# A strided-slice copy: gpsimd's transfers go over four batches, 1 MB each, and the hardware queues load eight pairs in place of six

## The chip, the cores and the metric

One core of one Trainium2 chip. The metric is the device time of one execution in microseconds (us). A run is an execution; most kernels here have three to nine runs, the four that measure one kind of transfer have one (state unknown). Runs more than 1.5% above the fastest of the same kernel count as slow and are left out of the ratios. A ratio is always the mean time of one kernel's fast runs over that of the other's fast runs of the same rounds, so it is not quite the ratio of the medians that stand beside it. Each profile is of one execution. Sizes of a batch or a transfer (2 MB, 1 MB, 512 KB) are in powers of two; totals and GB/s are decimal.

The engines that compute (tensor, vector, scalar, gpsimd) do nothing here but issue transfers. The work is done by the core's 16 DMA engines. Transfers are put to them on three queues: those of sync and of scalar, called the hardware queues (q1 and q10 in the profile), and that of gpsimd (q0, which the profile calls software_dynamic). The profile records what they move in packets, here of 2 or 4 KB of data.

## The reference

```python
# x: (32, 1024, 512) float32, start 0, stop 512, stride 2
def reference(x, start, stop, stride):
    return x[:, start:stop:stride, :].astype(np.float32)
```

The result is 32 batches of 256 rows of 2 KB: row r of a batch is input row 2r. 16.78 MB are read and 16.78 MB written. A batch of the input is 2 MB, a batch of the output 0.5 MB, so two batches n apart are 2n MB apart in the input and n/2 MB in the output.

## The kernel before

Every batch is split into its even and its odd output rows. One half goes direct from input to output on gpsimd's queue; the other half is loaded into on-chip tiles ("held") and stored from there by sync. Which half goes direct is decided by `apart`.

```python
FIRST = 6

def apart(b):                        # parity of the rows of batch b that go direct
    return 1 - (b >> 1 & 1)

def two(t, b, step, parity):         # rows of one parity of batches b and b + step: 512 KB
    return t[b : b + step + 1 : step].rearrange("b (p two) d -> two p b d", two=2)[parity]

    # ...
    copied = [(g + b, step) for g in range(0, B, 8) for b, step in ((0, 5), (2, 5), (1, 3), (3, 3))]
    # ...
            for i in range(FIRST):                       # six pairs on the hardware queues
                (sp, act)[i % 2].dma_start(held[i], two(src, 2 * i, 1, 1 - apart(2 * i)))
            for n, (b, step) in enumerate(copied):       # 16 direct pairs, 10 held ones
                pool.dma_start(two(out, b, step, apart(b)), two(src, b, step, apart(b)))
                i = n + FIRST // 2
                if FIRST <= i < pairs:
                    pool.dma_start(held[i], two(src, 2 * i, 1, 1 - apart(2 * i)))
            order = [pairs - 3, *range(pairs - 3), pairs - 2, pairs - 1]
            for b in (2 * i + k for i in order for k in range(2)):   # 32 stores of 256 KB
                to = out[b].rearrange("(p two) d -> two p d", two=2)[1 - apart(b)]
                sp.dma_start(to, held[b // 2][:, b % 2])
```

The direct pairs are 3 or 5 batches apart. The parity hangs on bit 1 of the batch number: direct rows are odd in batches 0, 1, 4, 5, 8, ... and even in 2, 3, 6, 7, ... I call this the rule. The direct pairs (0,5), (2,7), (1,4), (3,6) and the held pairs (0,1), (2,3), ... are just pairs whose two batches agree in bit 1, so that one transfer can have one parity.

## Time and profile before

| | before |
|---|---|
| time, median (range) | 79.38 us (79.25 to 80.14), three runs |
| profiled span | 77.1 us |
| bytes moved by the DMA engines | 25.17 MB, mean 327 GB/s |
| sum of the queues' shares of 16 engines | 96.1% |
| gpsimd's transfers | 26 of 512 KB, up to 8 under way |
| hardware transfers | 6 loads of 512 KB, 32 stores of 256 KB |

The prediction shows the lines behind these numbers. In the view by stretches each line has the stretch in us from the span's start and its length, the time in which gpsimd was busy with instructions (and how many), the clock of the tensor engine (idle here), the share of the time in which the 16 DMA engines had a packet, and the bytes moved per time. The share can come out a little over 1, because a packet is counted whole in the stretch in which it starts and because packets overlap a little: in the records up to 22 are under way at once on the 16 engines. A DMA share of 1 beside a low rate means that the engines have work but their packets take long.

### The profile page before, as it was taken

The numbers are of one execution on the slowest core, as the hardware profiler recorded it, in microseconds if no ns is written. First come the engines' busy times: TensorE is split into PE (matmuls) and PEld (weight loads), VectorE is DVE, ScalarE is ACT, GpSimd is POOL, SyncE is SP. The second block draws the span as 40 slices with busy tenths as digits, with TensorE's granted clock in tenths as the row PEclk, the third lists the DMA queues.
The fourth block names the chain that finished last, engine by engine and source line by source line (L and its number), as shares of the span: only waits on it lengthen the run. The fifth ranks groups of instructions, "written<-read, shape, count | busy, mean of one in ns | idle before, by whom it ended". The sixth has DMA issues, their size and how long they took to land.

```text
span 77.1 us, 122 instructions
## 1 busy us (share of the span) xinstructions
POOL 18.6 (24%) x30
## 2 busy tenths in 40 slices
POOL 4996003213436333464633000000000000000000
DMA  0899999999996999999989999999999999999970
GB/s 9 263 303 310 298 310 314 354 327 389 381 327 238 372 340 310 378 378 417 330 319 361 317 342 358 384 333 338 406 406 405 358 350 371 349 350 357 358 245 7
DMA packets 9984, 25.17 MB, mean 327 GB/s; under 512 B 1024, under 2 KB 1024, under 8 KB 9984
## 3 DMA queue, kind: packets, MB, share of 16 engines
q0 software_dynamic: 3744, 13.63, 51.3%
q1 hardware_dynamic: 5424, 9.96, 37.7%
q10 hardware_dynamic: 816, 1.57, 7.1%
HBM read 16.78 MB, written 16.78 MB: 435 GB/s over the span
## 4 chain that ended last, share of the span: by engine, by line
DMA 48%; issue 3%; POOLq 1%; POOL 1%; PEldq 0%
DMA held<-in_x_dram 34%; DMA out_dram<-in_x_dram 14%; POOLq L77 1%; POOL out_dram L39 1%; PEldq L77 0%
## 5 line engine op out<-in xcount | busy, mean ns | idle before, releaser
L39 POOL DMA_DIRECT2D out_dram<-in_x_dram x16 | 11.2, 699 | 11.5 <-DMA out_dram<-in_x_dram 9.9
L42 POOL DMA_DIRECT2D held<-in_x_dram x10 | 7.3, 729 | 11.4 <-DMA out_dram<-in_x_dram 8.0
L63 POOL MEMSET const-float32-0.0<- 128x1 f32 x1 | 0.1, 98 | 0.2 <-issue 0.2
L63 POOL MEMSET const-bfloat16-1.0<- 128x1 bf16 x1 | 0.1, 102 | 0.0
L63 POOL MEMSET const-float32-1.0<- 128x1 f32 x1 | 0.1, 98 | 0.0
L63 POOL MEMSET const-uint8-127<- 128x1 uint8 x1 | 0.1, 98 | 0.0
## 6 DMA issues: line engine op xcount, KB each, us to landing
out_dram<-in_x_dram POOLq DMA_DIRECT2D x16, 512.0 KB, 13.0
out_dram<-held SPq DMA_DIRECT2D x32, 256.0 KB, 6.1
held<-in_x_dram POOLq DMA_DIRECT2D x10, 512.0 KB, 12.4
held<-in_x_dram SPq DMA_DIRECT2D x3, 512.0 KB, 11.2
held<-in_x_dram ACTq DMA_DIRECT2D x3, 512.0 KB, 12.2
```

The lines of the kernel that those rows point to most:

```text
L39: pool.dma_start(two(out, b, step, apart(b)), two(src, b, step, apart(b)))
L42: pool.dma_start(held[i], two(src, 2 * i, 1, 1 - apart(2 * i)))
L63: nc = _bacc.Bacc("TRN2", target_bir_lowering=False, num_devices=1)
L77: with _tile.TileContext(nc) as tc:
```

## The change

gpsimd's transfers go over four batches at once, 1 MB each, so that there are fewer of them and fewer waits; and eight pairs, not six, are loaded by the hardware queues, which then carry 40 transfers. The core of the diff:

```diff
-FIRST = 6
+EARLY = 4
+
+def batches(q):
+    first = q // 4 * 16 + q % 4
+    return [first + 4 * k for k in range(4)]
 
-def apart(b):
-    return 1 - (b >> 1 & 1)
+def apart(q):
+    return 1 - (q >> 1 & 1)
 
-def two(t, b, step, parity):
-    return t[b : b + step + 1 : step].rearrange(...)[parity]
+def part(t, q, parity, of=slice(0, 4)):
+    b = batches(q)[of]
+    return t[b[0] : b[-1] + 1 : 4].rearrange(...)[parity]
...
+            for q in range(EARLY):
+                for queue, of in ((nc.sync, slice(0, 2)), (nc.scalar, slice(2, 4))):
+                    queue.dma_start(held[q][:, of], part(src, q, 1 - apart(q), of))
+            direct(0, slice(0, 2))
+            direct(0, slice(2, 4))
+            direct(1)
+            load(4)
+            direct(2)
+            load(5)
+            direct(3)
+            direct(4)
+            load(6)
...
+            for q in [quads - 2, *range(quads - 2), quads - 1]:
+                for k, b in enumerate(batches(q)):
...
```

A quad q is the batches q, q+4, q+8, q+12 (or 16 more). Its batches share bit 1 with q, so `apart(q)` is the old rule for every batch, and the same rows go direct as before. That is also why the step is 4: of four equally spaced batches all agree in bit 1 only if the step is a multiple of 4.

More of the change, by code (lines that the diff above doesn't have):

```diff
@@ L3 @@
 from concourse import mybir
-FIRST = 6
-def apart(b):
-    return 1 - (b >> 1 & 1)
-def two(t, b, step, parity):
-    return t[b : b + step + 1 : step].rearrange("b (p two) d -> two p b d", two=2)[parity]
+EARLY = 4
[6 more added lines that the diff above has]
+    b = batches(q)[of]
+    return t[b[0] : b[-1] + 1 : 4].rearrange("b (p two) d -> two p b d", two=2)[parity]
 def kernel(tc, x, start, stop, stride, out):
@@ L29, with direct, load @@
     P = rows // 2
-    sp, act, pool = nc.sync, nc.scalar, nc.gpsimd
-    copied = [(g + b, step) for g in range(0, B, 8) for b, step in ((0, 5), (2, 5), (1, 3), (3, 3))]
-    pairs = B // 2
+    quads = B // 4
     with tc.tile_pool(name="io", bufs=1) as io:
-        held = [io.tile([P, 2, D], x.dtype, name=f"held{i}") for i in range(pairs)]
-        with tc.manual_schedule():
-            for i in range(FIRST):
-                (sp, act)[i % 2].dma_start(held[i], two(src, 2 * i, 1, 1 - apart(2 * i)))
-            for n, (b, step) in enumerate(copied):
-                pool.dma_start(two(out, b, step, apart(b)), two(src, b, step, apart(b)))
-                i = n + FIRST // 2
-                if FIRST <= i < pairs:
-                    pool.dma_start(held[i], two(src, 2 * i, 1, 1 - apart(2 * i)))
-            order = [pairs - 3, *range(pairs - 3), pairs - 2, pairs - 1]
-            for b in (2 * i + k for i in order for k in range(2)):
-                to = out[b].rearrange("(p two) d -> two p d", two=2)[1 - apart(b)]
-                sp.dma_start(to, held[b // 2][:, b % 2])
+        held = [io.tile([P, 4, D], x.dtype, name=f"held{q}") for q in range(quads)]
+        def direct(q, of=slice(0, 4)):
+            nc.gpsimd.dma_start(part(out, q, apart(q), of), part(src, q, apart(q), of))
+        def load(q):
+            nc.gpsimd.dma_start(held[q], part(src, q, 1 - apart(q)))
+        with tc.manual_schedule():
+            for q in range(EARLY):
[10 more added lines that the diff above has]
+            load(6)
+            direct(5)
+            load(7)
+            direct(6)
+            direct(7)
+            for q in [quads - 2, *range(quads - 2), quads - 1]:
+                for k, b in enumerate(batches(q)):
+                    to = out[b].rearrange("(p two) d -> two p d", two=2)[1 - apart(q)]
+                    nc.sync.dma_start(to, held[q][:, k])
 _INS = ['x', 'start', 'stop', 'stride']
```

## The prediction

> **What bounds the kernel now.** No engine computes anything: the kernel copies every second row of half of each batch, 16.78 MB read and 16.78 MB written. Half goes straight from input to output, half through on-chip tiles ("held"), so the DMA engines carry 8.39 MB three times over (direct, load, store): 25.17 MB. I read first the page's slices and its table of DMA queues.
>
> ```profile
> DMA  0899999999996999999989999999999999999970
> ...
> DMA packets 9984, 25.17 MB, mean 327 GB/s; under 512 B 1024, under 2 KB 1024, under 8 KB 9984
> ...
> q0 software_dynamic: 3744, 13.63, 51.3%
> q1 hardware_dynamic: 5424, 9.96, 37.7%
> q10 hardware_dynamic: 816, 1.57, 7.1%
> ```
>
> The queues' shares sum to 96.1% of 16 engines' span: the DMA engines never rest. q0 is gpsimd's queue, q1 that of sync (three loads, all 32 stores), q10 that of scalar (three loads). The first question about any wait here is therefore whether it ever leaves a DMA engine without work, so I next read the stretches.
>
> ```profile
> core 0: us, POOL busy (x), PEclk, DMA share, GB/s
> 2.00:6.00 4.00, 4.00 (x7) 1.00 0.93 285
> 6.00:18.00 12.00, 2.38 (x4) 1.00 0.99 323
> 18.00:42.00 24.00, 11.32 (x16) 1.00 1.02 348
> 42.00:54.00 12.00, 0.00 (x0) 1.00 1.00 345
> 54.00:60.00 6.00, 0.00 (x0) 1.00 1.05 405
> 60.00:74.00 14.00, 0.00 (x0) 1.00 1.07 355
> ```
>
> From 6 us on the DMA share is 0.99 or more in each. What differs is GB/s, that is, how long one packet takes. The stages are: hardware loads alone (2 to 6), hardware loads beside gpsimd's transfers (6 to 18), gpsimd alone (18 to 42), gpsimd beside stores (42 to 54), stores alone (54 on). The waits of gpsimd come last:
>
> ```profile
> POOL out_dram L39 <- DMA out_dram<-in_x_dram: 9.9, 9, 1.9
> POOL held L42 <- DMA out_dram<-in_x_dram: 8.0, 2, 5.4
> POOL held L42 <- DMA held<-in_x_dram: 3.4, 6, 0.7
> ```
>
> They sum to over 20 us, and the order of instructions shows why: eight transfers go out at once, and each later one waits for the one eight before it. This wait looks as if it were to be won. The stretch 18 to 42, in which nearly all of it falls, says no: the share there is 1.02, since eight transfers of 512 KB (4.2 MB, 12 us at 348 GB/s) stand in the queue while gpsimd waits.
>
> What the time consists of, from the packet records. A 2 KB packet of the hardware queues takes 84 ns undisturbed (the median from 54 to 60 us), a 4 KB packet of gpsimd's queue 159 ns (its median). The means over the run are longer: 13.63 MB in 4 KB packets are 3328, and 51.3% of 77.1 us times 16 over 3328 is 190 ns (some 9 ns a completion packet included); likewise 96 ns in q1 and 114 ns in q10. Undisturbed, the data packets would take (3328 x 159 + 5632 x 84)/16 = 62.6 us. The remaining 11 us of the 74 us are stretching: in the records 6.2 us in q0, 3.2 in q1, 1.4 in q10. In q0 it sits in few packets: 90% take under 194 ns, the worst 1% over 800, and while they last the other queues' packets of that engine stand still. So the bound is how memory answers a mix of reads and writes, not the issue.
>
> **What the Trainium skill says.** "DMA: Bandwidth & Descriptors", section Issuing engines are not separate DMA queues: transfers of all issuers run on the same 16 engines and interleave, and issuing from several only saves issue time. The trace agrees: 16 engines are full at 0.99 to 1.02 with one queue and with three. The same page, section Measured, gives 341 GB/s for 1 MB and asks for at least 1 MiB per transfer. That is for a transfer which stands alone; with eight in the queue this trace gets 348 from 512 KB ones, so I expect nothing from size as such. The same page, section SWDGE vs HWDGE vs iDMA, says that a packet of gpsimd's queue is preferably at most 4096 B. Here all are 4096 B, with two rows of 2 KB in each instruction's inner dimension; no run yet shows whether four rows make one packet of 8 KB. Last, its section Latency and other measured facts has a row on HBM row pitches of large powers of two (a pitch of 2 MiB 164 GB/s, 4 and 8 MiB 103, in copies between HBM tensors). The kernel before pairs batches 1, 3 or 5 apart (2, 6, 10 MB in the input); the new one puts batches 4 apart, 8 MB, into one transfer. No trace of before shows what that costs.
>
> **The change, part by part.**
>
> *Fewer and larger gpsimd transfers.* 26 of 512 KB become 13: two of 512 KB and eleven of 1 MB, 12.58 MB in all. gpsimd has up to 7 MB under way where it had 4.2, and only the last five of 13 wait for a completion. Issue: 26 at 0.70 or 0.73 us become 11 at perhaps double that, the same 18 us or less, all beside the transfers. Removed wait: 0 us on the path, as the engines were full. Completion packets: 26 x 16 become 13 x 16, 208 fewer at 9 ns on 16 engines, 0.1 us gained. The first transfer stays at 512 KB, so the start at 6.4 us (first packet of q0) stays.
>
> *Packet size.* From 84 ns for 2 KB and 159 for 4 KB: 9 ns fixed and 75 ns for each 2 KB, so 8 KB would be an estimated 309 ns (the few 8 KB packets before the kernel's start take 307 at the least). 3072 packets of 4 KB at 159 are 30.5 us of 16 engines, 1536 of 8 KB at 309 are 29.7: 0.8 us gained, if it happens. I give it 4 in 10, so 0.3 us. If stretching comes per packet, part of q0's 6.2 us could go as well; I add 0.4 us for that.
>
> *Two more pairs on the hardware queues.* 1.05 MB of loads move from q0 to q1 and q10. The stage with three queues gets longer: there the hardware queues and q0 share about equally (0.94 + 1.03 MB against 1.91 from 6 to 18 us), so about 2.1 MB go at 323 instead of 348 GB/s: 6.5 - 6.0 = 0.5 us lost.
>
> *When stores start.* The first store waits for pair 13 (at 42.1 us) before, for quad 6 after. Ahead of it on gpsimd's queue stood 11 direct and 8 load transfers, 9.96 MB, and 3.15 MB of hardware loads: 13.1 MB. Now it is 5 direct and 3 load quads, 8.39 MB, and 4.19: 12.6 MB. At 0.33 MB/us that is 1.6 us earlier, less the 0.5 above: near 41 us. As all engines are full before and after, an earlier start saves nothing by itself; it moves 0.5 MB of gpsimd's traffic from before the stores to beside them. Both stages run at 345 to 348, so 0 us. The 40 hardware transfers make five rounds of eight; the stores' waits for the store eight before change nothing while eight of 256 KB are queued (share 1.07 from 60 to 74).
>
> Sum: -0.1 - 0.3 - 0.4 + 0.5 = -0.3 us. The plan by stage agrees: 12.58 MB are left at 41 us, at the 0.36 MB/us that the rest now runs at (12.06 MB from 42.1 to 75.6 us) they end at 76 us. I lean a little further to faster, 0.3 us more, because the deeper queue lets an engine that was held up by a long packet catch up later instead of holding up the next issue: 78.8 us.
>
> **The rivals.**
>
> *The waits were real.* The slice with 6 and the low stretch of 22 to 26 us (286 GB/s in the view of that stretch) look like a drained queue. Against it: the longest packet of the run, 2.1 us, starts there, and the records fill the 16 engines at 15.9 or more throughout when each packet is spread over its duration; a starved engine would have none. If I am wrong, the 18 to 42 stage at perhaps 375 GB/s would save 24 x (1 - 348/375) = 1.7 us: 77.5 us.
>
> *The 8 MB step hurts.* For it: stretching is only in stages that read, and its packets come in groups (7 to 10 over 400 ns within half a us), as of collisions in memory. Against it: the engines work on different rows at any time, and the same bytes are moved. A q0 stretch half as long again would be 3.1 us: 82 us. I hold a quarter of that size likelier.
>
> *The write-only tail is the bound.* From 60 us stores run at 355 GB/s against 405 from 54 to 60, with nothing else under way. I don't know why. If stores four batches apart stay at 405, some 5 MB gain 1.7 us: 77.5. If large gpsimd packets take 4 parts of 5 beside the stores, the store-only tail grows by about 1 MB, and nothing is lost as long as it runs at 355.
>
> **Range and chances.** A first-order sum near zero, an upside of 1 to 2 us from packets, stalls or the tail, a downside of 1 to 3 us from the pitch: 77.2 to 80.5 us. Two per cent are 1.6 us, so faster means below 77.8 us: 0.28, since two of the upsides can add up. Slower means over 81 us: 0.14. The rest, 0.58, is within.
>
> **What would show it.** DMA share still 0.99 or more from 6 us on, and gpsimd's waits far below 20 us without a matching gain: then the removed wait was hidden. The count of q0's packets: 3280 (4 KB) or 1744 (8 KB). The end of the hardware loads at about 25 us instead of 19, the first store near 41. The mean of a q0 packet per byte over 190 ns per 4 KB: the pitch hurts. GB/s of the last 15 us away from 355: the order of stores matters. I am wrong if the share was already full and the time still moves by over 2% without one of these.

## The result, and the profile after

The changed kernel took 108.56 us (median of six runs, 107.63 to 109.54) against 79.19 us of before in the same rounds (six runs, 78.65 to 80.14). The ratio of the fast runs is 1.367, with a 95% interval of 1.358 to 1.377: slower by 37%. The prediction of 78.8 us (77.2 to 80.5) was wrong.

The page of the kernel after, slices and table of queues (packets, MB, share of 16 engines' span):

```profile
DMA  1999989899879899998989999989998669999961
...
DMA packets 10064, 25.17 MB, mean 237 GB/s; under 512 B 848, under 2 KB 848, under 8 KB 10064
...
q0 software_dynamic: 3280, 12.58, 50.0%
q1 hardware_dynamic: 5696, 10.49, 29.8%
q10 hardware_dynamic: 1088, 2.10, 9.1%
```

The bytes are the same 25.17 MB. The shares sum to 88.9% of a span of 106.2 us, so packets took 94.4 us of 16 engines, where they took 96.1% of 77.1, that is 74.1 us, before: 20.3 us more. The engines were empty for 11.8 us in place of 3.0: 8.8 us more. Together these are the 29.1 us. q0's 3280 packets are 3072 of data, still 4 KB each, and 208 for completions. In time per data packet, worked out as in the prediction (share times 106.2 us times 16, over the data packets), q0 went from 190 to 277 ns and q10 from 114 to 151, while q1, which mostly stores, went from 96 to 99.

The view by stretches of the kernel after, chosen where the rate changes:

```profile
core 0: us, POOL busy (x), PEclk, DMA share, GB/s
2.00:8.00 6.00, 5.26 (x8) 1.00 0.92 149
8.00:22.00 14.00, 0.76 (x1) 1.00 0.93 221
22.00:26.00 4.00, 0.75 (x1) 1.00 1.01 354
26.00:40.00 14.00, 0.76 (x1) 1.00 0.90 183
...
44.00:60.00 16.00, 0.74 (x1) 1.00 0.90 182
...
90.00:104.00 14.00, 0.00 (x0) 1.00 0.94 336
```

The first line is the most telling. From 2 to 8 us nothing runs but the loads of the hardware queues (the first packet of q0 starts at 9.2 us). They are pairs of 512 KB as before, on the same two queues, yet they move 149 GB/s (160 from 2 to 6 us) where the kernel before has 285 from 2 to 6 us. No large transfer and no third queue can be at fault there, and not the eight loads in place of six either (t2 below has eight, and moves 278 from 2 to 6 us). What is new in these loads is their batches: 0 and 4 on sync, 8 and 12 on scalar, where before there were 0 and 1, 2 and 3. Later the rate jumps between some 182 and some 350 GB/s, with the engines full or nearly so in both.

The waits of gpsimd in the kernel after (in total us, times, longest):

```profile
POOL held L45 <- DMA out_dram<-in_x_dram: 15.8, 2, 9.6
POOL out_dram L42 <- DMA held<-in_x_dram: 9.7, 1, 9.7
POOL out_dram L42 <- DMA out_dram<-in_x_dram: 8.3, 2, 5.3
```

There are 5 waits in place of 18 (17 in the lines shown of before, and one of 0.8 us), and they sum to 33.8 us in place of 22.1. Fewer waits did not make less waiting: a wait lasts 6.8 us in the mean where it lasted 1.2. The first store, issued at 42.1 us before, is issued at 64.1.

A last difference is in the trace's completion records. A transfer completes on 16 engines one by one. Before, the first and the last of the 16 are 0.8 to 2.8 us apart; in the changed kernel the direct transfers over quads 6 and 7 have 16.8 and 17.5 us between them (66.0 to 82.8 and 68.8 to 86.3 us). The engines had drifted far apart. When the next issue, a store's too, waits for the slowest one, the quick ones can run empty. I take the 8.8 us for that; it is argued and not tested.

### The profile page after: what moved, and what is told of

The parts are those of the page before. It is cut to its first block, busy times and chain, and to the rows that moved or that the text cites. A ratio compares the mean times of both kernels' runs of the same rounds, so it can differ in the third digit from the quotient of the medians.

```text
span 106.2 us, 106 instructions
## 1 busy us (share of the span) xinstructions
POOL 10.0 (9%) x17
## 2 busy tenths in 40 slices
DMA packets 10064, 25.17 MB, mean 237 GB/s; under 512 B 848, under 2 KB 848, under 8 KB 10064
## 3 DMA queue, kind: packets, MB, share of 16 engines
q0 software_dynamic: 3280, 12.58, 50.0%
## 5 line engine op out<-in xcount | busy, mean ns | idle before, releaser
L42 POOL DMA_DIRECT2D out_dram<-in_x_dram x9 | 6.7, 751 | 18.9 <-DMA held<-in_x_dram 9.7
L45 POOL DMA_DIRECT2D held<-in_x_dram x4 | 3.0, 761 | 15.8 <-DMA out_dram<-in_x_dram 15.8
```

The lines of the kernel that those rows point to most:

```text
L42: nc.gpsimd.dma_start(part(out, q, apart(q), of), part(src, q, apart(q), of))
L45: nc.gpsimd.dma_start(held[q], part(src, q, 1 - apart(q)))
```

## The experiments

The theories at the start were these. **A:** batches 4 apart, 8 MB in the input, collide in memory. **B:** size and depth (1 MB, up to 7 MB under way) let the engines drift, and that costs. **C:** the larger share of the hardware queues costs. Three more came up on the way: **E**, neighbouring transfers of one parity collide; **G**, its form with the length of data of one parity in a row; and **H**, the one that stood.

### 1. Adjacent batches in the changed kernel

```diff
-    first = q // 4 * 16 + q % 4
-    return [first + 4 * k for k in range(4)]
+    return [4 * q + k for k in range(4)]
...
-    return t[b[0] : b[-1] + 1 : 4]...
+    return t[b[0] : b[-1] + 1]...
```

> The changed kernel with one thing undone: a quad is four adjacent batches (2 MB apart in the input, 0.5 MB in the output) in place of four batches 4 apart (8 MB and 2 MB). Sizes, queues, order and waits stay as in the changed kernel. Theory A (the 8 MB step makes the accesses of one transfer collide in memory): back to about 79 us, within 2 of the kernel before. Rival B (1 MB transfers and up to 7 MB under way let the 16 engines drift apart, and the drift costs): stays at about 108 us. Rival C (the longer stage with three queues): stays above 100 us.

Measured: 89.38 us against 79.45 of before, ratio 1.127 (1.116 to 1.138). It is neither 79 nor 108: on the face of it the step carries some 19 us, and some 10 are left. Stretches of this run (37 to 46 us is mostly direct copies, 46 to 50 a load, 70 to 84 stores alone):

```profile
core 0: us, POOL busy (x), PEclk, DMA share, GB/s
...
37.00:46.00 9.00, 0.00 (x0) 1.00 1.02 226
46.00:50.00 4.00, 0.00 (x0) 1.00 1.02 288
...
70.00:84.00 14.00, 0.00 (x0) 1.00 1.06 406
```

The loads recovered in part. The direct copies did not, though the engines are full (1.02), and the stores became faster than in the kernel before (355). So what is left sits in the direct copies.

### 2. Batches 4 apart in the kernel before

All pairs 4 apart; only the direct ones; only the held ones:

```diff
-    copied = [... for b, step in ((0, 5), (2, 5), (1, 3), (3, 3))]
+    copied = [... for b, step in ((0, 4), (2, 4), (1, 4), (3, 4))]   # e2, e3
...
-    two(src, 2 * i, 1, 1 - apart(2 * i))
+    two(src, low(i), 4, 1 - apart(low(i)))    # e2, e4: low(i) = i // 4 * 8 + i % 4
```

> The kernel before with its transfers of 512 KB, its 26 + 38 split and its order, but every pair is of two batches 4 apart, the direct ones (before 3 or 5 apart) and the held ones (before adjacent). Theory A: slow, 95 to 110 us, with stretches under 200 GB/s. Rivals B and C: within 2% of 79 us.

> The kernel before with only the direct pairs 4 apart; loads stay adjacent. Theory A: slower, some part of the 29 us, I guess 10 to 15 us, in the stretches where direct transfers run (6 to 54 us); the first 6 us, in which only hardware loads run, stay at about 285 GB/s. Rivals B and C: 79 us.

> The kernel before with only the held pairs (loads, and the order of the stores) 4 apart; direct pairs stay 3 or 5 apart. Theory A: slower, I guess by 10 to 15 us, with the first 6 us near 150 GB/s as in the changed kernel. If the loads alone make the cost, e4 has all of it and e3 none. Rivals B and C: 79 us.

Measured: all pairs 94.26 us (four runs, 90.73 to 95.40; three of them count as slow, but even the fastest is 11 us over before). Direct only 85.36 us, ratio 1.075 (1.067 to 1.083). Held only 83.68 us, ratio 1.055 (1.046 to 1.063). In these kernels the step of 4 is in the old sizes, the old 26 and 38 transfers and the old order of transfers (with the held pairs, the batches are also stored in another order), and it alone costs 6, 4 and at least 11 us. That is A. My guesses of 10 to 15 us for each part were too high, and the first 6 us of e4 were not at 150 GB/s: two pairs 4 apart, on two queues, started at 181 GB/s (2 to 4 us) and went on at 345 (4 to 6 us).

### 3. Loads alone, then stores alone

A kernel that only loads, in quads of 1 MB on gpsimd's queue, and then only stores; the result is still right.

```python
quads  = [([4 * q + k for k in range(4)], 0) for q in range(4)]         # 1 apart, even rows
quads += [([16 + q + 4 * k for k in range(4)], 0) for q in range(4)]    # 4 apart, even rows
quads += [([q + 5 * k for k in range(4)], 1) for q in range(5)]         # 5 apart, odd rows
quads += [([20 + q + 3 * k for k in range(4)], 1) for q in range(3)]    # 3 apart, odd rows
```

> All 16.8 MB are loaded on gpsimd's queue in quads of 1 MB and nothing else runs: batches 1 apart, 4 apart, 5 apart, 3 apart. Then all is stored by sync in four orders: parity changing every two batches as in the kernel before; one parity, batches in sequence; one parity, batches 4 apart; parity changing again. Theory A: loads 1, 5, 3 apart over 350 GB/s, 4 apart under 250. Stores: as the run with adjacent quads showed 406 GB/s and the kernel before 355, I expect 355 with changing parity and 406 with one parity in sequence; 4 apart open, 340 if the order of the changed kernel slows stores by itself, 406 if its stores were slow only because the engines had drifted apart.

One run, correct. The stretches of the loads: 1 apart, the first quad 4 apart, the other quads 4 apart, 5 and 3 apart.

```profile
core 0: us, POOL busy (x), PEclk, DMA share, GB/s
4.00:16.00 12.00, 5.56 (x8) 1.00 0.98 327
17.00:22.00 5.00, 0.75 (x1) 1.00 0.97 168
22.00:36.00 14.00, 2.24 (x3) 1.00 1.00 307
36.00:56.00 20.00, 0.75 (x1) 1.00 1.00 328
```

With nothing else under way, in one queue and at one size, the first four batches 4 apart load at half the rate of batches 1, 3 or 5 apart. Then the rate recovers within the same stage. In the completion records the engines are 0.9 us apart at the fourth load, 0.8 at the fifth (the slow one) and 6.1 at the eighth. So the stage 4 apart sets off the drift; that the drift in turn makes the recovery, as engines no longer touch the same rows of the four batches at the same moment, is not shown, and the rate is up from 22 us, with the engines still 0.8 us apart. The loads 1, 3 and 5 apart were expected over 350 GB/s and came at 327 and 328. The stores by themselves were at 373 GB/s as a whole, and 4 apart they were no slower than in other orders (381 against 376 and 377 with a parity that changes every two batches, 392 in sequence; 355 and 406 were expected). So reads alone show A, and stores of one batch each do not. Whether a direct copy also pays for writing to batches 4 apart is not separated.

### 4. Direct copies alone

The whole result by direct copies on gpsimd's queue, nothing else running; pairs (m1) with steps 1, 4, 3 and 5, 2, and quads (m2) with steps 1, 4, 5, 3, each stage with one parity.

> Another kernel with the same result: everything goes direct on gpsimd's queue in pairs of 512 KB, nothing else runs. Four stages of 4.2 MB, each of 16 batches and one parity: pairs 1 apart, 4 apart, 3 and 5 apart (as in the kernel before), 2 apart. Theory A in its first form (only the 8 MB input step collides): 1, 3/5 and 2 apart at about 330 GB/s, 4 apart near 180 to 230. After the run with adjacent quads a second form (A2): adjacent direct copies, 0.5 MB apart in the output, collide too: 1 apart under 280 GB/s and only 3/5 apart at 330 or more. Rival B (drift from deep queues): all four stages alike.

> The same with quads of 1 MB: batches 1 apart, 4 apart, 5 apart, 3 apart. A2: 1 apart near 215 GB/s (as the direct stages of the run with adjacent quads), 4 apart near 180, 5 and 3 apart at 320 or more. Rival B (size): all four slow, under 250, and slower than the pairs of the same step.

One run each: 91.35 and 90.78 us. Both expectations missed. Outside a slow patch at the start of the stages 4 apart (123 GB/s from 23 to 28 us in the pairs), the stretches were mostly at some 170 to 250 GB/s, those with the steps 3 and 5 of the kernel before included. Pairs and quads did not differ, which speaks against B. But why were pairs 3 and 5 apart so slow here, when the kernel before moves 345 GB/s from 42 us on with the same pairs? I saw that each stage had kept one parity, and formed theory E. That the stages had also given up the rule I overlooked.

### 5. Quads with odd steps

The changed kernel with quads 5 apart (batches 0 to 19) and 3 apart (20 to 31):

```diff
-    first = q // 4 * 16 + q % 4
-    return [first + 4 * k for k in range(4)]
+    first, step = (q, 5) if q < 5 else (q + 15, 3)
+    return [first + step * k for k in range(4)]
```

> The changed kernel with quads of batches 5 apart (the first 20 batches) and 3 apart (the last 12) in place of 4 apart: sizes, queues, order and waits of the changed kernel, odd steps as in the direct pairs of the kernel before. Theory A2: the whole loss is the step, so 78 to 80 us. Rival B (size and depth keep a cost of their own, as the 10 us left with adjacent quads could say): 85 to 92 us.

Measured: 89.98 us, ratio 1.127 (1.113 to 1.142). The same 10 us are left as with adjacent batches. So a special virtue of the steps 3 and 5 is not it. The number lies in rival B's range; experiment 7 tests B.

### 6. Parity: alternating, or in runs

A direct-only kernel (m4) with four stages: pairs 3 and 5 apart as in the kernel before, parities in turn; adjacent quads in turn; the same pairs' other halves, in runs of one parity; the quads' other halves in runs. And three kernels with another parity:

```diff
-    return 1 - (b >> 1 & 1)      # i1: the kernel before
+    return 1 - (b >> 3 & 1)
...
-    return 1 - (q >> 1 & 1)      # i3: the changed kernel; i4: the kernel of experiment 5
+    return q & 1
```

> Everything direct on gpsimd's queue, same result, four stages of 4.2 MB: pairs 3 and 5 apart whose parity (even or odd output rows) alternates from transfer to transfer; adjacent quads, alternating; the same pairs in runs of four of one parity; the same quads in runs of two of one parity. The two runs of direct copies showed some 215 GB/s for every step while each stage kept one parity, the kernel before 340 with alternating ones. Theory E (neighbouring transfers of one parity collide): first stage 320 to 350, second 280 to 340, third about 215, fourth 215 to 250. Rival F (direct copies without loads beside them are always this slow): all four about 215.

> The kernel before with one number changed: the half that is copied directly changes after eight batches, not after two; so eight neighbouring batches' transfers have one parity. Sizes, steps, queues and order stay. Theory E: the reading stages fall to 220 to 300 GB/s, the stores alone rise to 405: 85 to 92 us. Rivals (size, depth or queue share made the 10 us that odd quads kept): 77 to 80 us.

> The changed kernel with its parity alternating from quad to quad; the batches stay 4 apart. Theory E together with A (both cost, about 10 us the runs of one parity and 19 the step): 95 to 101 us. If the step alone made all of it: 108. If parity alone: 80.

> Quads 5 and 3 apart and parity alternating from quad to quad: both suspected costs taken from the changed kernel, its 1 MB transfers, 40 hardware transfers and order kept. Theories A and E together: 77 to 80 us, as the kernel before. If size or depth cost by themselves: 83 to 90.

Measured: i1 91.76 us, ratio 1.150 (1.138 to 1.162); i3 109.66 us, ratio 1.381 (1.369 to 1.394); i4 89.69 us, ratio 1.126 (1.116 to 1.136). On record these three verdicts are "unclear"; in these rounds three of the seven runs of before count as slow (80.4 to 80.8 us), which is far less than the differences read here. The stretches of the direct-only kernel's stages:

```profile
core 0: us, POOL busy (x), PEclk, DMA share, GB/s
4.00:17.00 13.00, 7.12 (x11) 1.00 0.98 283
20.00:36.00 16.00, 2.07 (x3) 1.00 0.96 215
40.00:56.00 16.00, 2.99 (x4) 1.00 0.96 165
62.00:78.00 16.00, 0.00 (x0) 1.00 1.01 219
```

i1 looked like a triumph for E: one number changed in `apart`, 12 us lost at 512 KB. But i4 alternates from transfer to transfer and is no better than experiment 5, and i3 no better than the changed kernel. E could only be saved by saying that 1 MB of one parity in a row is already too much (G).

### 7. Size or order: halves in turn and halves crossed

The kernel i4 with every 1 MB transfer on gpsimd's queue cut into two of 512 KB, in the same order (i7), or crossed with the halves of the neighbour, which has the other parity (i8):

```diff
-            direct(1)
-            load(4)
...
+            for two in plan:      # ((direct, 0), (direct, 1)), ((load, 4), (direct, 2)), ...
+                for what, q, of in ((w, q, of) for w, q in two for of in halves):     # i7
+                for what, q, of in ((w, q, of) for of in halves for w, q in two):     # i8
+                    what(q, of)
```

> The kernel with odd quads and parity alternating by quad (89.7 us), each 1 MB transfer of gpsimd's queue cut into two of 512 KB issued one after the other: the order of the data stays, runs of one parity are still 1 MB; only size and depth (4.2 MB under way, not 7) go back to those of the kernel before. If the size or the depth of the transfers costs the 10 us: 78 to 81 us. If the length of one parity in a row costs them: 87 to 91 us.

> The same halves, but crossed: first half of one transfer, first half of the next (other parity), second half, second half. The parity changes every 512 KB. If the length of one parity in a row is the cause: 78 to 82 us, and 8 us or more under the halves in turn. If it is the size: as the halves in turn. If neither: both stay at 87 to 91.

Measured: in turn 88.65 us, ratio 1.119 (1.113 to 1.126); crossed 88.27 us, ratio 1.113 (1.108 to 1.118). Against the 1.126 of i4, a size of 1 MB and the deeper queue cost about half a microsecond, within the intervals: B falls, where the step is not 4. The order of parities costs nothing: G falls, and E with it.

The completion records say the same of the drift. The largest time between the first and the last of a transfer's 16 engines is 2.1 to 3.2 us in the kernels with 1 MB transfers and odd steps or adjacent batches (e1, i2, i4, i6). It is 10.0 to 12.8 us in the kernel before with a step of 4 in 512 KB transfers (e2, e3, e4), and 17.5 and 17.2 in the changed kernel and i3. Of all twenty kernels, the eight in which some transfer has a step of 4 lie at 7.4 us or more, the other twelve at 5.4 or less. So the drift comes with the step, not with size or depth.

### 8. Is it the parity at all?

The kernel before with both parities inside each transfer (the second batch of a pair takes the rows of the other parity), and i4 with the batches split into first and second half of their rows in place of even and odd rows:

```diff
-    return t[b : b + step + 1 : step].rearrange(...)[parity]
+    ap = [[2 * row, 128], [step * batch + (1 - 2 * parity) * row, 2], [1, t.shape[2]]]
+    return bass.AP(t.tensor, t.offset + b * batch + parity * row, ap)    # i5, apart(b) = 1 - (b & 1)
...
-    rearrange("b (p two) d -> two p b d", two=2)[parity]
+    rearrange("b (two p) d -> two p b d", two=2)[parity]                 # i6
```

> The kernel before with both parities inside every transfer (the second batch of a pair takes the other rows than the first), direct and held. If what counts is that both parities are under way at every moment: 74 to 79 us, with reading stages over 350 GB/s. If the engines work in step, so that all are at the same batch of the pair at once, or if the parity stands for something else: 85 or more.

> The kernel with odd quads and alternating halves (89.7 us), a batch being split into the first and the second 128 rows in place of even and odd rows; so one transfer covers every output row of its range, and every second 4 KB of input is no longer skipped. If the remaining 10 us come from one parity using only a part of the addresses: 76 to 82 us. If the rows' pattern does not matter: 88 to 91.

Measured: mixed pairs 97.08 us, ratio 1.224 (1.218 to 1.230); row halves 89.43 us, ratio 1.126 (1.118 to 1.133). Mixing makes it worse, and dropping the parity split changes nothing. In the mixed pairs the hardware loads by themselves are slow already, though their batches are adjacent:

```profile
core 0: us, POOL busy (x), PEclk, DMA share, GB/s
2.00:6.00 4.00, 4.00 (x7) 1.00 0.88 161
```

The kernel before has 285 there, the changed one 160. The two rows that such a load takes beside each other are 2 MB and 4 KB apart in the input, in place of 2 MB. So a step of 4 is not the only way to slow a load; which rows go together counts.

I then listed for every kernel which rows of which batches it copies directly. The kernels of 88 to 92 us, and the mixed pairs, have one thing in common: half of their direct rows break the rule. The kernel before and the changed one break it nowhere. In m4 the first stage (283 GB/s) obeys it everywhere, the third (165) breaks it everywhere, and the other two (215, 219) are half and half. This is theory H: a direct copy is slow when its row's parity equals bit 1 of its batch number.

### 9. The rule reversed; and the hardware pairs alone

```diff
-    return 1 - (b >> 1 & 1)      # t1
+    return b >> 1 & 1
...
-FIRST = 6                        # t2
+FIRST = 8
```

> The kernel before with the rule reversed: the odd rows go direct where bit 1 of the batch number is 1, the even ones where it is 0. Sizes, steps, queues, order, and the alternation of parity stay. Theory H (a direct copy collides with itself in memory, reads with writes, when the row's parity equals bit 1 of the batch number): direct stages fall to some 165 to 200 GB/s, 95 to 110 us. Rival (alternation or symmetry: the two halves are alike): within 2% of 79 us. Rival K (mixing the two kinds costs, a pure rule either way is good): 79 us too.

> The kernel before with eight pairs loaded by the hardware queues in place of six, so that 40 transfers use these; all else as before. This is one part of the change alone. The prediction had 0.5 us lost: 79.9 us, within 2%. If the larger share on the hardware queues matters for the loss: over 82 us.

Measured: t1 103.43 us against 79.13, ratio 1.301 (1.290 to 1.312). This kernel has every size, step, queue and place in the order of the kernel before, and the parity still alternates; only the two halves of every batch have changed roles. The stretches of its profile (of a run that counts as slow by 1.9%):

```profile
core 0: us, POOL busy (x), PEclk, DMA share, GB/s
2.00:6.00 4.00, 4.00 (x7) 1.00 0.93 296
6.00:18.00 12.00, 1.92 (x4) 1.00 0.97 224
18.00:42.00 24.00, 6.19 (x9) 1.00 0.98 214
...
84.00:98.00 14.00, 0.00 (x0) 1.00 1.06 362
```

In this kernel loads alone (296) and stores alone (362) run as before (285 and 355). Every stage with direct copies in it is slow, with full engines. So H is shown as far as the relation goes: at the sizes and steps of before, direct rows that all obey the rule give 79 us, half of them 92 (i1; 97 where both kinds are in every transfer), none of them 103. The rival that a pure rule is good either way falls with it. That it is the reads and writes of the copies that meet in memory is argued: in t1 loads alone and stores alone do not care, only stages in which direct copies run. The mixed pairs, whose loads alone are slow, show that this is not all there is to it.

t2: 79.50 us, ratio 1.000 (0.990 to 1.011). The larger share of the hardware queues costs nothing: C falls.

No kernel of the eighteen beats the one before; t2 equals it.

## Why the prediction was wrong

**What held.** The kernel is bound by how long its packets take, not by issue, and the removed waits were worth nothing. The repairs show this best: with the fewer and larger transfers but without the step of 4 (i4), nothing was gained over the same data in halves (experiment 7). Its own sign for the pitch came too: q0's packets went over 190 ns, to 277. The part "two more pairs on the hardware queues" was taken at 0.5 us lost; alone it measured nothing, within 1%.

**Packet size.** "Four in ten" for 8 KB packets: the count is 3280, so all stayed at 4 KB, though eleven of the thirteen instructions had four rows of 2 KB in their inner dimension, and the 0.3 and 0.4 us of gain that hung on it were not there. "DMA: Bandwidth & Descriptors", section SWDGE vs HWDGE vs iDMA, has packets of preferably at most 4096 B; this agrees. The issue of a 1 MB transfer took 0.75 us, not double the 0.70 to 0.73 of a 512 KB one.

**The step that failed** is in the rival "The 8 MB step hurts": "Against it: the engines work on different rows at any time, and the same bytes are moved. ... I hold a quarter of that size likelier". The mechanism was named, with the right page and the right sign. The size was off: the rival's 3.1 us was an invented half of q0's stretching, and the sum had no term for it at all. Measured in its place: packets took 20.3 us more of 16 engines. q0 alone is (277 - 190) ns times 3072 over 16, or 16.7 us: over the median of 159 ns, its stretching went from 6.2 us to 22.4, and not to half as much again. Another 8.8 us are engines left empty. The argument from "the same bytes" was false in kind. Loads alone, of the same bytes and shape, start at 168 or run at 327 GB/s by their step (experiment 3). I had also put the step on gpsimd's transfers only, when it also came to the hardware pairs, whose first 6 us dropped to 149 GB/s.

**"The deeper queue lets an engine ... catch up later"**, for which I took 0.3 us: the engines did not catch up. They drifted up to 17.5 us apart, and the share fell to 0.90; the prediction had 0.99 or more. The depth is not what did it: with the same depth and no step of 4 they stay within 3.2 us (experiment 7). The hardware loads ended at 38.6 us and the first store was issued at 64.1, where the prediction had about 25 and 41.

**Readings that were off.** Of gpsimd's 22.1 us of waits only 12.3 fall in the stretch 18 to 42 us, not "nearly all"; 9.8 fall before, where the share is 0.99, so the conclusion stands. Stretching was not "only in stages that read": from 60 us on, with stores alone, the median 2 KB packet takes 93 ns in place of 84, some 2 us in all. And the "plan by stage" (76 us, where the last data packet of before landed at 75.6) points to 0.4 us slower, not with the sum to 0.3 faster.

**What the diff could have told.** The steps 3 and 5 and the `apart` of the kernel before are worth 6 us (e3) and 24 us (t1), and I took them for bookkeeping. The change kept the second and so had to give up the first: four equally spaced batches agree in bit 1 only with a step that is a multiple of 4 (8 was not tried). Conversely every repair of the step (experiments 1, 5) gave up the rule and fell 10 us short. At this transfer size, with one parity and equal spacing, the two cannot both be had.

**What stays open.** Pairs 4 apart cost at least 11 us (experiment 2), the changed kernel 29. The other 18 or fewer may come from four such batches in a transfer in place of two, from two hardware queues that read 8 MB apart at once, or from the drift that follows; size by itself (experiment 7, without the step) and queue share (t2) are excluded, the rest is not separated. Breaking the rule as well (i3) left the changed kernel where it was (1.381 against 1.367, intervals that overlap), so the two costs do not add up, and I don't know why. Why the mixed pairs (97 us) are worse than the other kernels with half their direct rows against the rule (88 to 92) is known only in part: their loads alone are slow from the start.

## What to carry to other kernels

When DMA engines are full but move different rates in different stages, look at which addresses are under way together, before size, depth or queue. A change that only "batches" transfers also changes their strides; test it by loading the old stride in the new size, and the new stride in the old size. And odd-looking constants in a tuned copy kernel (steps of 3 and 5, a parity from one bit of an index) should be reversed once on the chip before they are taken for bookkeeping: one sign was worth 24 us here.

## What the Trainium skill lacked or had wrong

- "DMA: Bandwidth & Descriptors", section Latency and other measured facts, row on HBM row pitches: it covers a pitch between partitions of HBM to HBM copies, with 164 GB/s at 2 MiB and 103 at 4 and 8 MiB. Here the pitch is between the batches of one transfer: loads 8 MB apart started at 168 GB/s, those 2, 6 and 10 MB apart moved 327 or 328. The row is right in kind for 8 MB; no loss showed at 2 MB, but hardware loads with a pitch of 2 MB and 4 KB moved 161 GB/s in place of 285 (mixed pairs). That the loss can fade within a stage (307 GB/s after the first load) and that the engines drift apart with it (7.4 to 17.5 us against 5.4 or less) is not in it.
- No page has that a copy from HBM to HBM depends on which rows it copies: the same pairs moved 283 GB/s with one choice of rows and 165 with the opposite one, and the whole kernel took 79 or 103 us.
- The same page, section Measured, has the rule to batch to 1 MiB or more. With eight transfers in the queue, cutting 1 MB transfers into 512 KB ones changed the ratio to before from 1.126 to 1.119: the rule bought nothing here.
- No page has that stores alone change their rate with nothing else under way: 405 GB/s from 54 to 60 us and 355 from 60 to 74 in the kernel before. In the kernel before every stored row has the parity of bit 1 of its batch number; where only half of them had it, stores stayed at 406 (experiment 1). Whether that is the cause is not shown.
